# One input sum of a seven-product projection loaded after the last scores, and the second rope's scaling moved to ScalarE

## The chip, the cores and the metric

The kernel runs on one core of a Trainium2 chip. The metric is the time of one execution on the device in microseconds. Three runs of the kernel before gave 515.02, 515.41 and 516.37 us, so the median is 515.41 us. Engines are named as in the profile: PE is TensorE, PEld its weight loads, DVE VectorE, ACT ScalarE, POOL GpSimd and SP SyncE, from whose queue most transfers are issued.

## The reference

One decoder block over 512 tokens of 1024 channels, in float32. A projection of the normed input feeds two mixers: a sparse attention (compressed, selected and sliding branches) and a multi-scale retention of four heads, run in four chunks of 128 tokens. Their outputs are gated, merged, projected and added to the input. What matters here is the retention, and that attention's work precedes it:

```python
h = rms_norm(x, norm_pre)
proj = h @ w_in                              # 1024 -> 6936
(q_n, k_c, v_c, k_s, v_s, k_w, v_w, g_n, z_n,
 q_r, k_r, v_r, z_r, m_a, m_b) = jnp.split(proj, split_points(), axis=-1)
...
o_a = nsa_sequence(...)                      # attention, 8 heads of 64
y_a = (o_a * jax.nn.silu(z_n)) @ w_nsa_o
q_r = apply_rotary(q_r.reshape(B, S, 4, 128), ret_ang)
k_r = apply_rotary(k_r.reshape(B, S, 4, 128), ret_ang) * 128 ** -0.5
# retention, per chunk of 128 tokens and head:
att = jnp.einsum('nihd,njhd->nhij', qc, kc) * decay_mask
o = att @ v + (q * q_dec) @ state            # then state = decay * state + k^T v, o normalized
y_b = (o_b * jax.nn.silu(z_r)) @ w_ret_o
merged = jax.nn.sigmoid(m_a) * y_a + jax.nn.sigmoid(m_b) * y_b
return x + rms_norm(merged @ w_out, norm_post)
```

## The kernel before

A float32 product is made of three matmuls: each operand x is split into a high half `hi` in the matmul's reduced type (a copy, mostly on ACT, L200) and a low half `lo = x - hi` (a subtraction, mostly on DVE, L212), and PE adds hi·hi, hi·lo and lo·hi in one PSUM bank (`mm3`, whose matmuls are L233; transposes are L237). The normed and transposed input lies in `hTh` and `hTl`. Weights come from HBM through a ring of four `raw` tiles of 128 x 1024 (loads on SP, L373), and each half of a `raw` tile is split into `whi` and `wlo`, rings of nine. Working buffers are carved out of two large tiles: `arena_f` (float32) and `arena_r` (the matmul's type). `nat` is a ring of four tiles of 128 x 512 for intermediate results, `bank` a PSUM bank.

The program goes through a plan: after the first projections come the attention's blocks, then for the first pair of retention heads the rope (`QK`), values (`VR`) and gates, then `QZ2`: queries, keys and gates of the second pair of heads are computed in a Strassen-like way from seven products of half-size matrices instead of eight. Their names in the code are 11, s2 (with weight sum T2), s1 (T1), 22 (T4), 12, s4 and s3 (T3); those with an s need a sum of quarters of the input. The sums of the input (`hs` in DRAM) and of the weights (`wqT` and, for the later merge, `wmT`) are made by copies and accumulating transfers in DRAM on SP and POOL (L425, L434). `load_sum` brings an input sum into `arena_r`: one transfer from SP (L511), ACT makes the high half in place and the negated high half beside it (four steps of 128 x 512), and POOL issues a transfer that adds the source to the latter, which gives the low half. `free_at` says after which event the sum's buffer may be written. For the sum s2 (`qs2`) the buffer is the 8 KB of `arena_r` in which the low halves of the attention's keys, `kB`, lie; `att_head`, which issues the scores of one head and one block of 128 queries against `kA` and `kB`, is called 48 times.

`tail_qk` (L1134) is what follows the rope's products of one tile of 128 tokens. For the second pair of heads (`hp` = 1) it has a `base`: the tile's last product is added to an earlier partial sum (L212, `nat<-bank,arena_f`), and then four scaled products on half of the tile each (L225; a row's scale `rs` times the tile times the cosine or sine) and two combining steps (L212, `nat<-nat,nat`) give the roped queries and keys. PE transposes them (L237), ACT and DVE split them into halves, and `ret` computes the chunk's scores, masks them (ACT copies the scores' second half from the bank, DVE adds and masks, ACT makes the high half `ah`), multiplies them with the values and updates the state. `load_rtab` (L1132) loads the tables of cosine and sine, and the masks come at L1096 when the attention ends.

The order of all instructions on all queues is fixed when the program is built. A planner, `Order`, keeps a planned time for each engine and a list of generators, each of which says at what planned time and on which engine its next piece may go. The planner always records the piece that is first by those times. A piece which says that its data arrive later is therefore recorded later and placed further back on its engine's queue; what a piece is waiting for on the chip has no part in it. `e = od.dma(...)` is the planned landing of a transfer, and `yield e, "act"` hands the next piece to ACT's list with that time.

```python
    free_at = {"ms1": "ret13", "ms2": "MB0", "ms3": "P2", "ms4": "P1",
               "qs2": "att", "qs1": "vr01", "qs4": "qs2end", "qs3": "qs1end"}
```

Of the kernel before, what the change touches and what calls it, by code (L numbers as in the profile page):

```python
# [14 lines left out]
OP = mybir.AluOpType  # L15
# [3 lines left out]
P = 128  # L19
# [128 lines left out]
def block_kernel(ctx: ExitStack, tc, x, xT, g_pre, ws, small, w2s, norm_post, rope_r, dmask, out):  # L148
# [21 lines left out]
    def f(ap):  # L170
        return ap.bitcast(FT)
# [3 lines left out]
    od = Order()  # L175


    def size(a):
        n = 1
        for k in a.shape[1:]:  # L180
            n *= k
        return n
# [4 lines left out]
    def near(*aps):  # L187
        return not any(far(a) for a in aps)

    def act_ns(o, i, k=0):  # L190
        return 0.833 * size(o) + (51 if far(i) else 93) + 93 * k
# [4 lines left out]
    def lazy(*vals):  # L196
        return sum(v is not None and not isinstance(v, (int, float)) for v in vals)

    def act(o, i, func=AF.Copy, r=0.0, **kw):
        S.activation(o, i, func, **kw)  # L200
        return od.op("act", act_ns(o, i, lazy(kw.get("bias"), kw.get("scale"))) + (95 if "accum_out" in kw else 0), r)
# [9 lines left out]
    def tt(o, a, b, op, r=0.0, e="dve"):  # L211
        (V if e == "dve" else G).tensor_tensor(o, a, b, op=op)  # L212
        if op == OP.pow:
            return od.op(e, 300 + 164 * size(o), r, True)
        return od.op(e, (1.042 * size(o) + 69) if e == "dve" else (2.36 * size(o) + 77), r, e == "pool" or near(o, a, b))
# [8 lines left out]
    def stt(o, a, s, b, op0, op1, r=0.0):  # L224
        V.scalar_tensor_tensor(o, a, s, b, op0=op0, op1=op1)  # L225
        return od.op("dve", 1.042 * size(o) + 69 + 61 * lazy(s), r, near(o, a, b))
# [5 lines left out]
    def mm(ps, a, b, start, stop, r=0.0, cost=None):  # L232
        T.matmul(ps, a, b, start=start, stop=stop)  # L233
        return od.pe(cost or max(0.4418 * size(b) + 1, 107 if a.shape[-1] > 64 else 54), r, a.dtype == FT)

    def tr(ps, a, idn, r=0.0):
        T.transpose(ps, a, idn)  # L237
        return od.pe(58 if a.dtype == FR else 107, r, a.dtype == FT)
# [6 lines left out]
    def sub_split(lo, src, hi, r, e="dve"):  # L245
        return tt(lo, src, f(hi), OP.subtract, r, e)
# [98 lines left out]
    def h_quart(n):  # L345

        if n[0] == "q":
            return SQ[n in ("qs1", "qs3")]
        n = n.removeprefix("m")
        if n == "s1":  # L350
            return S1H, S1L
        k, c = hq[n]
        return hTh[:, k:k + 4, half[c]], hTl[:, k:k + 4, half[c]]

    free_at = {"ms1": "ret13", "ms2": "MB0", "ms3": "P2", "ms4": "P1",
               "qs2": "att", "qs1": "vr01", "qs4": "qs2end", "qs3": "qs1end"}

    def in_ring(p):

# [24 lines left out]
    nxt, freed = [0], {}  # L384
# [108 lines left out]
    def load_sum(key):  # L493

        yield od.need(free_at[key], "sum" + key[1:])
        r = max(freed[free_at[key]], sumr[id(hsum[key[1:]])])
        hi, lo = h_quart(key)
        src = hsum[key[1:]].rearrange("(p k c) -> p k c", p=P, k=4)
        yield r
        if key in ('qs3', 'qs4', 'ms2', 'ms3', 'ms4'):  # L500
            DMA.dma_start(f(lo), src)
            e = od.dma(P * 4096, r)
            for c in (slice(0, 2), slice(2, 4)):
                yield e, "act"
                act(hi[:, c], f(lo[:, c]), r=e)
            for c in (slice(0, 2), slice(2, 4)):
                yield od.eng["act"], "dve"
                sready[key] = sub_split(lo[:, c], f(lo[:, c]), hi[:, c], od.eng["act"])
            od.flags.add(key)
            return  # L510
        DMA.dma_start(f(hi), src)  # L511
        e = od.dma(P * 4096, r)
        for c in (slice(0, 2), slice(2, 4)):
            yield e, "act"
            act(hi[:, c], f(hi[:, c]), r=e)
            yield e, "act"
            ea = act(lo[:, c], f(hi[:, c]), r=e, scale=-1.0)
        ea = max(ea, adder[0])
        yield ea
        G.dma_start(lo.rearrange("p k c -> p (k c)"), src.rearrange("p k c -> p (k c)"), accum_op=OP.add)  # L520
        sready[key] = od.op("pool", 1000.0, ea) + 7000.0
        adder[0] = sready[key]
        od.flags.add(key)
# [124 lines left out]
    def rs(t, i=0):  # L648
        return rs3[:, i, t:t + 1]
# [310 lines left out]
    def att_head(t, g, brs, j, slot):  # L960

        L, nb, h, b0 = P * (t + 1), len(brs), g * 4 + j, brs[0]
        s = yield from PS.get()
        sv = s[:, 0:nb * L].rearrange("p (b c) -> p b c", b=nb)
        q = qT[t][:, h, :]
        mm(sv, q, kA[:, b0:b0 + nb, g, 0:L], True, False)
        e = mm(sv, q, kB[:, b0:b0 + nb, g, 0:L], False, True)
        yield e, "dve"

        Pj = slot["P"]  # L970
        pv = Pj[:, 0:nb * L].rearrange("p (b c) -> p b c", b=nb)
        nm, z = ((slot["stat"][:, i, j * nb:(j + 1) * nb]) for i in range(2))
        for b in range(nb):
            V.tensor_tensor_reduce(pv[:, b, :], sv[:, b, :], maskp[:, 512 - L:512], 1.0, -NEG, OP.add, OP.min,
                                   nm[:, b:b + 1])
            od.op("dve", 1.04 * L + 80, e)
        e = od.op("dve", 80)
        PS.put(s, e)
        yield e, "act"
        for b in range(nb):  # L980
            e = act(pv[:, b, :], pv[:, b, :], AF.Exp, r=e, bias=nm[:, b:b + 1], scale=-1.0, accum_out=z[:, b:b + 1])
        slot["pv"], slot["z"] = pv, e

    def att_norm(t, g, brs, slots):

# [137 lines left out]
    rtr = [0.0] * 8  # L1123

    def rtab_of(i):

        return rtab if i < 4 else zt[0][i - 4]

    def load_rtab(i, r):
        rtr[i] = od.dma(P * 2048, r)  # L1130
        od.flags.add(f"rt{i}")
        DMA.dma_start(rtab_of(i), rope_r[i // 4, i % 4 * P:(i % 4 + 1) * P, :])  # L1132

    def tail_qk(hp, t, ps, e, base=None):  # L1134
        yield od.need("q0", "q1", "q2", "q3", "cmp0", "cmp1", f"rt{4 * hp + t}")
        tv = rtab_of(4 * hp + t).rearrange("p (s a c) -> p s a c", s=2, a=4)
        t1 = yield from NAT.get()
        t2 = yield from NAT.get()
        v1 = t1.rearrange("p (a r c) -> p a r c", a=4, r=2)
        v2 = t2.rearrange("p (a r c) -> p a r c", a=4, r=2)  # L1140
        pv = v1 if base else ps.rearrange("p (a r c) -> p a r c", a=4, r=2)
        if base:
            u, given, then, *more = base
            yield od.need(given, *more)
            yield max(e, kept[given]), "dve"
            e = tt(t1, ps, u, OP.add, max(e, kept[given]))
            then(ps, e)
        yield max(e, rtr[4 * hp + t]), "dve"
        if not base:
            for i in range(2):  # L1150
                e = stt(v1[:, :, i, :], pv[:, :, i, :], rs(t), tv[:, 0], OP.mult, OP.mult, e)
            yield e, "dve"
        stt(v2[:, :, 0, :], pv[:, :, 1, :], rs(t), tv[:, 1], OP.mult, OP.mult, e)
        e = stt(v2[:, :, 1, :], pv[:, :, 0, :], rs(t), tv[:, 1], OP.mult, OP.mult, e)
        if base:
            yield e, "dve"
            for i in range(2):
                e = stt(v1[:, :, i, :], pv[:, :, i, :], rs(t), tv[:, 0], OP.mult, OP.mult, e)
        else:
            ACC.put(ps, e)  # L1160
        if hp == 0 and t < NT - 1:
            load_rtab(t + 1, e)
        yield e, "pool"
        tt(v1[:, :, 0, :], v1[:, :, 0, :], v2[:, :, 0, :], OP.subtract, e)
        e = tt(v1[:, :, 1, :], v1[:, :, 1, :], v2[:, :, 1, :], OP.add, e)
        NAT.put(t2, e)
        pt = yield from PT.get()
        yield e + PE_LAG
        act(kf[t], t1[:, 256:512], r=e)
        for a in range(4):  # L1170
            e = tr(pt[:, a * P:(a + 1) * P], t1[:, a * P:(a + 1) * P], ident)
        NAT.put(t1, e)
        yield e, "act"
        e = act(qk_h[t], pt, r=e)
        yield e, "dve"
        e = sub_split(qk_l[t], pt, qk_h[t], e)
        PT.put(pt, e)
        kr[t] = e
        od.flags.add(f"qk{hp}{t}")
# [60 lines left out]
    def pair_qz():  # L1240
# [18 lines left out]
        def keys(i, ps, e):  # L1259
            od.spawn(tail_qk(1, i, ps, e, (XA[i], f"qw{i}", free)), 1)  # L1260
# [589 lines left out]
    r = raws[0][1] - 600  # L1850
    for c in (slice(0, P), slice(P, SEQ)):
        e = act(hTh[:, 0, c], xTf[0][:, c], r=xTr[0], scale=gp[:, 0:1])
# [12 lines left out]
    for key in free_at:  # L1865
        od.spawn(load_sum(key), 1)
# [103 lines left out]
```

## Time and profile before

| What | Value |
|---|---|
| Median of three runs | 515.41 us (515.02 to 516.37) |
| Profiled execution | 515.82 us |
| Its span, first to last instruction | 513.9 us |
| Mean granted clock of PE | 0.996 |
| PE busy | 502.6 us (98%) |
| DVE busy | 424.2 us (83%) |
| ACT busy | 310.5 us (60%) |
| POOL busy | 49.7 us (10%) |

A line of the timeline gives the start and the length in microseconds, the engine, the line of the kernel, the operation, output and inputs, the shape and the number of instructions; a bracket at its end gives the engine's idle time just ahead and what ended it. A line of the grouped views has the count, then busy time in all and the mean in nanoseconds, then idle time ahead and its releasers. In the list of waits the numbers are total, times and longest. In the list of transfers the numbers are the size of one and the microseconds from its issue to its landing. Matmuls overlap, so that the start of the next one tells what one costs, not its length.

### The profile page before, as it was taken

To read this page: it belongs to the slowest core of one execution; us is meant where nothing else is said; L and a number is where in the kernel's file an instruction comes from. 1 tells how busy PE (TensorE), PEld (TensorE's weight loads), DVE (VectorE), ACT (ScalarE), POOL (GpSimd) and SP (SyncE) were. 2 spreads that over 40 slices of the span, in tenths; PEclk is the share of its full clock that TensorE was granted. 3 is DMA by queue.
4 is the path that set the end of the run, shared out by engine and by line. 5 is a ranking of instruction groups with operands and counts; after the bars stand their busy time and mean duration, and the time that the engine had idled before them with its cause. 6 is when DMAs were issued, how large, how long until landed. Compare 5 with 4: busy or idle time off the path is not lost.

```text
span 513.9 us, 7898 instructions
## 1 busy us (share of the span) xinstructions
PE 502.6 (98%) x2700; PEld 429.4 (84%) x2700; DVE 424.2 (83%) x987; ACT 310.5 (60%) x672; POOL 49.7 (10%) x82
## 2 busy tenths in 40 slices
PE   8999999999999999999999999999999999999994
PEld 7888789788888888888788887888888999888884
DVE  6699689979879789996689799786757789969887
ACT  5688579766568769575486575644614544427541
POOL 2000100000010000010131010113000000000011
PEclk9999999999999999999999999999999999999998
DMA  8997656702955732469669987185995997714825
GB/s 322 367 327 211 185 120 211 240 2 82 310 104 120 220 67 83 140 147 348 165 184 276 352 272 246 22 258 173 329 284 129 322 311 266 192 51 144 267 61 144
DMA packets 34248, 103.47 MB, mean 201 GB/s; under 512 B 3600, under 2 KB 8080, under 8 KB 34192
## 3 DMA queue, kind: packets, MB, share of 16 engines
q1 hardware_dynamic: 29312, 85.41, 46.3%
q0 software_dynamic: 4752, 17.30, 19.5%
q8 instruction: 21, 0.34, 0.3%
q10 hardware_dynamic: 144, 0.26, 0.1%
q14 instruction: 19, 0.16, 0.1%
HBM read 98.76 MB, written 34.08 MB: 259 GB/s over the span
## 4 chain that ended last, share of the span: by engine, by line
PE 80%; DVE 9%; DMA 5%; ACT 4%; issue 1%; SPq 0%; DVEq 0%; ACTq 0%
PE bank L233 75%; PE bank L237 5%; DMA arena_r<-hs 3%; DVE arena_f L212 2%; DVE wlo L212 2%; DVE arena_r L212 2%; ACT arena_r L200 2%; DMA raw<-in_stream_dram 1%; DVE nat L212 1%; ACT whi L200 1%; ACT nat L200 1%; DMA arena_f<-in_xT_dram 1%; DVE nat L225 1%; DVE arena_f L225 1%; ACT arena_f L200 0%
## 5 line engine op out<-in xcount | busy, mean ns | idle before, releaser
L200 ACT ACTIVATE whi<-raw 128x512 fp32r<-128x512 f32 x177 | 105.2, 627 | 53.7 <-PE bank L233 34.4
L212 DVE TENSOR_TENSOR wlo<-raw,whi 128x512 fp32r<-128x512 f32 x196 | 128.0, 686 | 9.2 <-ACT whi L200 6.5
L233 PE MATMUL bank<-whi,hTh 128*128 128x512 f32 x248 | 96.2, 403 | 0.3 <-ACT hTh L200 0.3
L233 PE MATMUL bank<-whi,hTl 128*128 128x512 f32 x248 | 93.3, 392 | 0.0
L233 PE MATMUL bank<-wlo,hTh 128*128 128x512 f32 x248 | 93.1, 391 | 0.0
L233 PE MATMUL bank<-arena_r 128*128 128x256 f32 (+2 forms) x328 | 69.5, 337 | 1.2 <-ACT arena_r L200 1.2
L233 PE MATMUL bank<-hTh,whi 128*128 128x512 f32 (+1 forms) x192 | 66.4, 346 | 0.0
L233 PE MATMUL bank<-arena_r,whi 128*128 128x512 f32 (+1 forms) x224 | 64.9, 374 | 0.0
L233 PE MATMUL bank<-hTh,wlo 128*128 128x512 f32 (+1 forms) x192 | 64.9, 338 | 0.0
L233 PE MATMUL bank<-hTl,whi 128*128 128x512 f32 (+1 forms) x192 | 64.9, 338 | 0.0
L233 PEld LDWEIGHTS bank<-arena_r 128*128 128x128 f32 x328 | 50.6, 189 | 7.7 <-ACT arena_r L200 1.6
L233 PEld LDWEIGHTS bank<-whi,hTl 128*128 128x128 f32 x248 | 46.5, 188 | 10.3 <-DVE hTl L225 0.3
L200 ACT ACTIVATE arena_r<-bank 128x512 fp32r<-128x512 f32 (+2 forms) x76 | 41.9, 569 | 21.6 <-PE bank L237 21.3
L233 PEld LDWEIGHTS bank<-whi,hTh 128*128 128x128 f32 x248 | 46.6, 188 | 9.1 <-ACT hTh L200 0.9
L233 PEld LDWEIGHTS bank<-wlo,hTh 128*128 128x128 f32 x248 | 46.7, 188 | 8.3
L200 ACT ACTIVATE arena_f<-arena_f,stat 128x384 f32<-128x384 f32 (+3 forms) x87 | 47.7, 560 | 8.2 <-DVE stat L212 4.6
L212 DVE TENSOR_TENSOR arena_r<-bank,arena_r 128x512 fp32r<-128x512 f32 (+2 forms) x68 | 43.7, 653 | 7.6 <-ACT arena_r L200 7.1
L233 PEld LDWEIGHTS bank<-arena_r,whi 128*128 128x128 f32 x224 | 41.0, 188 | 7.4
L233 PE MATMUL bank<-whi,arena_r 128*128 128x512 f32 (+1 forms) x152 | 44.7, 358 | 0.0
L233 PE MATMUL bank<-arena_r,wlo 128*128 128x512 f32 (+1 forms) x112 | 41.9, 374 | 0.0
L233 PEld LDWEIGHTS bank<-hTh,wlo 128*128 128x128 f32 x192 | 36.5, 190 | 4.0
L233 PEld LDWEIGHTS bank<-hTh,whi 128*128 128x128 f32 x192 | 36.5, 190 | 2.8
(160 smaller groups left out, 770.1 us busy)
## 6 DMA issues: line engine op xcount, KB each, us to landing
raw<-in_stream_dram SPq DMA_DIRECT2D x73, 512.0 KB, 4.8
arena_f<-in_xT_dram SPq DMA_DIRECT2D x16, 256.0 KB, 6.6
wqT<-in_stream_dram POOLq DMA_DIRECT2D x8, 512.0 KB, 5.4
raw<-wqT SPq DMA_DIRECT2D x8, 512.0 KB, 6.2
wmT<-in_stream_dram POOLq DMA_DIRECT2D x8, 512.0 KB, 7.4
woT<-in_stream_dram POOLq DMA_DIRECT2D x8, 512.0 KB, 7.6
raw<-wmT SPq DMA_DIRECT2D x8, 512.0 KB, 6.4
raw<-woT SPq DMA_DIRECT2D x8, 512.0 KB, 3.8
```

Source lines behind the costliest of these rows:

```text
L200: S.activation(o, i, func, **kw)
L212: (V if e == "dve" else G).tensor_tensor(o, a, b, op=op)
L225: V.scalar_tensor_tensor(o, a, s, b, op0=op0, op1=op1)
L233: T.matmul(ps, a, b, start=start, stop=stop)
L237: T.transpose(ps, a, idn)
```

## The change

Two edits. First, the flag on which the transfer of `qs2` waits is no longer the end of the attention but a new one, `scored`, which is set when the 48th `att_head` has recorded its score matmuls. The planned landing of that transfer gets 3000 ns more (the expression stands in both branches of `load_sum`, but `qs2` goes through the second alone). Second, `tail_qk` with a `base` no longer uses `rs` on DVE: ACT multiplies the sum by `rs` in place, DVE makes two plain products with the sine table (256 columns each) and one with the cosine table over all 512 columns, and the two combining steps stay. The tiles of the first pair are computed as before.

```diff
--- before.py
+++ after.py
@@ -353,7 +353,7 @@
         return hTh[:, k:k + 4, half[c]], hTl[:, k:k + 4, half[c]]
 
     free_at = {"ms1": "ret13", "ms2": "MB0", "ms3": "P2", "ms4": "P1",
-               "qs2": "att", "qs1": "vr01", "qs4": "qs2end", "qs3": "qs1end"}
+               "qs2": "scored", "qs1": "vr01", "qs4": "qs2end", "qs3": "qs1end"}
 
     def in_ring(p):
 
@@ -499,7 +499,7 @@
         yield r
         if key in ('qs3', 'qs4', 'ms2', 'ms3', 'ms4'):
             DMA.dma_start(f(lo), src)
-            e = od.dma(P * 4096, r)
+            e = od.dma(P * 4096, r) + (3000.0 if key == "qs2" else 0.0)
             for c in (slice(0, 2), slice(2, 4)):
                 yield e, "act"
                 act(hi[:, c], f(lo[:, c]), r=e)
@@ -509,7 +509,7 @@
             od.flags.add(key)
             return
         DMA.dma_start(f(hi), src)
-        e = od.dma(P * 4096, r)
+        e = od.dma(P * 4096, r) + (3000.0 if key == "qs2" else 0.0)
         for c in (slice(0, 2), slice(2, 4)):
             yield e, "act"
             act(hi[:, c], f(hi[:, c]), r=e)
@@ -965,6 +965,10 @@
         q = qT[t][:, h, :]
         mm(sv, q, kA[:, b0:b0 + nb, g, 0:L], True, False)
         e = mm(sv, q, kB[:, b0:b0 + nb, g, 0:L], False, True)
+        heads.append(e)
+        if len(heads) == 48:
+            freed["scored"] = e
+            od.flags.add("scored")
         yield e, "dve"
 
         Pj = slot["P"]
@@ -980,6 +984,8 @@
         for b in range(nb):
             e = act(pv[:, b, :], pv[:, b, :], AF.Exp, r=e, bias=nm[:, b:b + 1], scale=-1.0, accum_out=z[:, b:b + 1])
         slot["pv"], slot["z"] = pv, e
+
+    heads = []
 
     def att_norm(t, g, brs, slots):
 
@@ -1138,25 +1144,27 @@
         t2 = yield from NAT.get()
         v1 = t1.rearrange("p (a r c) -> p a r c", a=4, r=2)
         v2 = t2.rearrange("p (a r c) -> p a r c", a=4, r=2)
-        pv = v1 if base else ps.rearrange("p (a r c) -> p a r c", a=4, r=2)
+        pv = ps.rearrange("p (a r c) -> p a r c", a=4, r=2)
         if base:
             u, given, then, *more = base
             yield od.need(given, *more)
             yield max(e, kept[given]), "dve"
             e = tt(t1, ps, u, OP.add, max(e, kept[given]))
             then(ps, e)
-        yield max(e, rtr[4 * hp + t]), "dve"
-        if not base:
+            yield e, "act"
+            e = act(t1, t1, r=e, scale=rs(t))
+            r = max(e, rtr[4 * hp + t])
+            yield r, "dve"
+            for i in range(2):
+                tt(v2[:, :, i, :], v1[:, :, 1 - i, :], tv[:, 1], OP.mult, r)
+            e = tt(v1, v1, tv[:, 0].unsqueeze(2).broadcast_to([P, 4, 2, 64]), OP.mult, r)
+        else:
+            yield max(e, rtr[4 * hp + t]), "dve"
             for i in range(2):
                 e = stt(v1[:, :, i, :], pv[:, :, i, :], rs(t), tv[:, 0], OP.mult, OP.mult, e)
             yield e, "dve"
-        stt(v2[:, :, 0, :], pv[:, :, 1, :], rs(t), tv[:, 1], OP.mult, OP.mult, e)
-        e = stt(v2[:, :, 1, :], pv[:, :, 0, :], rs(t), tv[:, 1], OP.mult, OP.mult, e)
-        if base:
-            yield e, "dve"
-            for i in range(2):
-                e = stt(v1[:, :, i, :], pv[:, :, i, :], rs(t), tv[:, 0], OP.mult, OP.mult, e)
-        else:
+            stt(v2[:, :, 0, :], pv[:, :, 1, :], rs(t), tv[:, 1], OP.mult, OP.mult, e)
+            e = stt(v2[:, :, 1, :], pv[:, :, 0, :], rs(t), tv[:, 1], OP.mult, OP.mult, e)
             ACC.put(ps, e)
         if hp == 0 and t < NT - 1:
             load_rtab(t + 1, e)
```

ACT's queue, around the last scores and the attention's end. The four `arena_r<-arena_r` rows are the steps on the first input sum, `nat`, `arena_f` and `arena_r<-bank` are tails of the attention and the first rope.

```order
 L200 ACTIVATE arena_r<-bank_88 128x512
-L200 ACTIVATE whi<-raw 128x512 x3
+L200 ACTIVATE whi<-raw 128x512
+L200 ACTIVATE arena_r<-arena_r 128x512 x4
+L200 ACTIVATE whi<-raw 128x512
 L200 ACTIVATE nat_110<-bank_90 64x512
 L200 ACTIVATE arena_f<-nat_107 128x256
 L200 ACTIVATE whi<-raw 128x512 x2
 L200 ACTIVATE arena_r<-bank_87 128x512
-L200 ACTIVATE whi<-raw 128x512 x3
-L200 ACTIVATE arena_r<-arena_r 128x512 x4
+L200 ACTIVATE whi<-raw 128x512 x4
```

The four steps moved from behind the last of these splits to a place eight splits and tail rows earlier.

SP's queue over the same stretch (`wqT` copies are sums of weights, `hs_137` is the first input sum, `in_rope_r` the rope tables, `in_dmask` the retention masks).

```order
 L425 DMA wqT_134<-wqT_130 64x2x1024
 L425 DMA wqT_135<-wqT_131 64x2x1024
-L1132 DMA arena_f<-in_rope_r_dram 128x512 x2
-L373 DMA raw<-in_stream_dram 128x1024 x2
-L1096 DMA arena_f<-in_dmask_dram 128x4x128
 L511 DMA arena_r<-hs_137 128x1024
+L1138 DMA arena_f<-in_rope_r_dram 128x512 x2
+L373 DMA raw<-in_stream_dram 128x1024
+L1102 DMA arena_f<-in_dmask_dram 128x4x128
+L373 DMA raw<-in_stream_dram 128x1024
 L425 DMA wmT_120<-in_stream_dram 64x2x1024
```

The sum's load moved ahead of two rope tables, two weight loads and the masks. On POOL its accumulating transfer correspondingly stands one accumulation into `wqT_135` earlier.

DVE's queue at the first two key tiles of the second pair, in the kernel before (`nat_108` is the first tile's sum, `nat_107` the second's, `rs_146` the row scales; `arena_f<-nat_110,arena_f` is a gate).

```order
L212 TENSOR_TENSOR nat_108<-bank_84,arena_f 128x512
L212 TENSOR_TENSOR wlo<-raw,whi 128x512
L225 SCALAR_TENSOR_TENSOR arena_f<-nat_110,arena_f 128x512
L225 SCALAR_TENSOR_TENSOR nat_109<-nat_108,rs_146,arena_f 128x4x64 x2
L212 TENSOR_TENSOR wlo<-raw,whi 128x512
L212 TENSOR_TENSOR nat_107<-bank_85,arena_f 128x512
L225 SCALAR_TENSOR_TENSOR nat_108<-nat_108,rs_146,arena_f 128x4x64 x2
L225 SCALAR_TENSOR_TENSOR nat_110<-nat_107,rs_146,arena_f 128x4x64 x2
L212 TENSOR_TENSOR nat_108<-nat_108,nat_109 128x4x64 x2
```

And in the changed kernel, at the same place:

```order
L212 TENSOR_TENSOR nat_108<-bank_84,arena_f 128x512
L225 SCALAR_TENSOR_TENSOR arena_f<-nat_110,arena_f 128x512
L212 TENSOR_TENSOR wlo<-raw,whi 128x512
L212 TENSOR_TENSOR nat_109<-nat_108,arena_f 128x4x64 x2
L212 TENSOR_TENSOR nat_108<-nat_108,arena_f 128x512
L212 TENSOR_TENSOR nat_107<-bank_85,arena_f 128x512
L212 TENSOR_TENSOR wlo<-raw,whi 128x512
L212 TENSOR_TENSOR nat_108<-nat_108,nat_109 128x4x64 x2
```

The scaled products became plain ones, the cosine product became one row of 512 columns and stands directly behind the sine products, and the second tile's products moved behind the first tile's end. ACT's scaling of `nat_108` stands between the add and the first product, on another queue.

## The prediction

> **What bounds the kernel now.** I read the page first: its engine table, then its tenths.
>
> ```profile
> span 513.9 us, 7898 instructions
> ...
> PE 502.6 (98%) x2700; PEld 429.4 (84%) x2700; DVE 424.2 (83%) x987; ACT 310.5 (60%) x672; POOL 49.7 (10%) x82
> ```
>
> PE works 98% of the span, so only the moments in which PE stands still can be won. The change leaves the matmuls as they are; what it can be worth is therefore bounded by PE's waits in the stretch it touches. The list of PE's waits comes next.
>
> ```profile
> PE bank L233 <- ACT arena_r L200: 1.2, 1, 1.2
> ...
> PE bank L237 <- DVE arena_f L688: 0.9, 1, 0.9
> PE bank L237 <- DVE nat L212: 0.6, 1, 0.6
> ```
>
> The middle one lies at the start of the program (L688, the norm), which the change does not reach. The other two are at 245 us and 309 us; PE's timeline, with the rows just ahead of each, gives their size.
>
> ```profile
> 244.04 0.39 PE L233 MATMUL bank<-wlo,hTh 128*128 128x512 f32 x1
> 244.27 0.39 PE L233 MATMUL bank<-whi,hTl 128*128 128x512 f32 x1
> 245.83 1.91 PE L233 MATMUL bank<-arena_r 128*128 128x256 f32 x12 [1.17 <-ACT arena_r L200]
> ...
> 308.11 0.39 PE L233 MATMUL bank<-whi,hTl 128*128 128x512 f32 x1
> 309.06 0.66 PE L237 MATMUL bank<-ident,nat 128*128 128x128 f32 x4 [0.56 <-DVE nat L212]
> ```
>
> A matmul of 512 columns starts 0.23 us after the one ahead of it (244.04 to 244.27). Between 244.27 and 245.83 there are 1.56 us, so 1.33 are lost; between 308.11 and 309.06 there are 0.95, so 0.72 are lost. The two together, 2.05 us or 0.4%, are the most that the change can win directly. The chain of waits tells what is behind the first one.
>
> ```profile
> 232.79 0.63 SPq L1096
> ...
> 233.47 5.96 DMA arena_r<-hs
> ...
> 245.36 0.42 ACT arena_r L200
> ...
> 245.83 1.20 PE bank L233 x6
> ```
>
> The sum for the second Strassen product is issued at 233.47, takes 5.96 us, and ACT's work on it follows; after that come the retention tile's own (245.36 is its last, the high half of the masked scores), and PE gets it at 245.83.
>
> **The change, first part: the sum goes earlier.** The buffer's low halves of the keys are read last by the last scores, not by the end of the attention.
>
> ```profile
> 214.60 0.40 PE L233 MATMUL bank<-arena_r 128*128 128x256 f32 x2
> ...
> 214.93 1.19 SPq L425 DMA_DIRECT2D wqT<-wqT  x2
> 219.53 9.17 SPq L1132 DMA_DIRECT2D arena_f<-in_rope_r_dram  x2
> ```
>
> These are the last scores on PE and SP's rows behind them. The load now stands after the two copies of 214.93 and ahead of the rope loads, so it is issued at about 216.2. Its transfer shares the engines with the two copies; the groups of issues in that stretch price it:
>
> ```profile
> wqT<-wqT SPq DMA_DIRECT2D x2, 512.0 KB, 5.2
> arena_r<-hs SPq DMA_DIRECT2D x1, 512.0 KB, 6.0
> ...
> arena_r<-hs SPq DMA_DIRECT2D x2, 512.0 KB, 8.3
> ```
>
> The last row is of 274 to 286 us, where the same kind of load met four weight loads. 216.2 + 6.0 to 8.3 gives a landing at 222 to 225. ACT's four steps now stand behind a split of about 227:
>
> ```profile
> 227.80 1.31 ACT L200 ACTIVATE whi<-raw 128x512 fp32r<-128x512 f32 x2 [0.50 <-PE bank L233]
> ...
> 235.32 0.63 ACT L200 ACTIVATE whi<-raw 128x512 fp32r<-128x512 f32 x1 [2.56 <-DMA raw<-in_stream_dram]
> 239.45 2.48 ACT L200 ACTIVATE arena_r<-arena_r 128x512 fp32r<-128x512 f32 x4 [3.50 <-DMA arena_r<-hs]
> ```
>
> So they start 2 us or more after the landing and wait for nothing. They cost 2.48 us of ACT time there instead of here; behind them stand the splits of 227.80 and later, whose weights PE needs only some microseconds on, and ACT idles 2.56 us at 235.32, which takes up the push. I cost that at nothing; if this cover were gone, at most 2.48 us would fall on a split that PE waits for. The idle time of 3.50 us ahead of 239.45 goes with them.
>
> What is then last for the retention tile? Its scores on PE, and ACT's copy of them.
>
> ```profile
> 241.26 0.57 PE L233 MATMUL bank<-arena_r 128*128 128x256 f32 x4
> ...
> 243.50 0.38 ACT L200 ACTIVATE arena_f<-bank 128x256 f32<-128x256 f32 x1
> ```
>
> The order has the scores some five matmuls of 0.23 us nearer to the front, so at about 240.0 (239.8 to 240.2). They take 0.41 (241.26 to 241.67, the next start), and from ACT's copy to the end of the high half it is 245.36 + 0.42 − 243.50 = 2.28 us: 242.5 to 242.9. PE would ask at 244.27 + 0.23 = 244.50, or three matmuls sooner where the tile's products now stand, 243.8. That leaves about 1 us, and the first stall goes: −1.33 us.
>
> SP also moves two rope loads, raw loads and the mask load behind this one issue: 0.50 us of SP each time, no more; the rope loads, which stood at 219.53 waiting for their buffers for most of 9.17 us, lose nothing. POOL's accumulating load of the sum passes ahead of one accumulation into the weights' sums; those are read at 290 us or later. Both at nothing. The 3 us added to the planned landing costs nothing by itself: it only places ACT's steps.
>
> **Second part: ACT scales.** The rope of the second pair, four tiles, before and after on DVE (grouped by form, 280 to 320 us):
>
> ```profile
> L225 DVE SCALAR_TENSOR_TENSOR nat<-nat,rs,arena_f 128x256 f32<-128x256 f32 x16 | 6.8, 481 | 0.0
> ...
> L212 DVE TENSOR_TENSOR nat<-nat,nat 128x256 f32<-128x256 f32 x8 | 3.0, 420 | 0.0
> ...
> L200 ACT ACTIVATE arena_f<-arena_f,rs 128x512 f32<-128x512 f32 x4 | 2.9, 717 | 2.3 <-DVE arena_f L212 2.3
> ```
>
> Four scaled products of 256 columns go; in their place come two plain products of 256 and one of 512. On DVE's timeline the step from one start to the next tells what each costs:
>
> ```profile
> 298.88 0.69 DVE L212 TENSOR_TENSOR nat<-bank,arena_f 128x512 f32<-128x512 f32 x1
> 299.48 0.68 DVE L212 TENSOR_TENSOR wlo<-raw,whi 128x512 fp32r<-128x512 f32 x1
> ...
> 302.67 1.67 DVE L225 SCALAR_TENSOR_TENSOR nat<-nat,rs,arena_f 128x256 f32<-128x256 f32 x4
> 304.25 0.76 DVE L212 TENSOR_TENSOR nat<-nat,nat 128x256 f32<-128x256 f32 x2
> 304.92 1.29 DVE L212 TENSOR_TENSOR wlo<-raw,whi 128x512 fp32r<-128x512 f32 x2
> ...
> 308.25 0.75 DVE L212 TENSOR_TENSOR nat<-nat,nat 128x256 f32<-128x256 f32 x2
> ...
> 318.29 0.75 DVE L212 TENSOR_TENSOR nat<-nat,nat 128x256 f32<-128x256 f32 x2
> ```
>
> Four scaled products in a row cost 1.58 us (302.67 to 304.25), two plain ones of 256 columns 0.67 (304.25 to 304.92), one of 512 columns 0.60 (298.88 to 299.48). So 1.58 − 1.27 = 0.31 us less on DVE for each tile, 1.2 us in all, and 4 × 0.717 = 2.9 us more on ACT (the form's row with `rs`, the gates' scaling of the same size), off PE's path as long as DVE has other work between the add and the first product.
>
> DVE's rows carry no idle time from 298.88 to 319.04 (318.29 + 0.75): it, not the data, sets when the tiles are ready. I call the start of the first add X (298.88 before). The second tile is ready 10.1 us after X now. After, by the order, there stand eleven full-width instructions (0.60 each) and four pairs (0.67) between the first add and that tile's end: 9.3 us. PE asks for it at 308.34 − 1.33 = 307.0. With X one stall earlier (297.55) it is ready at 306.9 and the stall goes; with X unmoved it is ready at 308.2 and PE waits 1.2.
>
> The last tile: ready 20.2 us after X now, and PE takes it at 319.58 with 0.5 us to spare. After, four savings of 0.31 come off, but a gate's product and three more subtractions, 2.2 us together, are placed ahead of it: 21.1 to 21.2 us. PE's wish is 319.58 less 2.05, plus three matmuls (0.69) and a group of scores (0.41) that now stand ahead: 318.63. With X = 297.55 it is ready at 318.7, even.
>
> So all hangs on X, which DVE's and ACT's work of 280 to 298 us sets:
>
> ```profile
> 261.79 0.42 DVE L208 CAST whi<-raw 128x512 fp32r<-128x512 f32 x1
> 262.12 0.69 DVE L212 TENSOR_TENSOR wlo<-raw,whi 128x512 fp32r<-128x512 f32 x1
> ...
> 285.83 1.29 DVE L212 TENSOR_TENSOR arena_r<-arena_r 128x512 fp32r<-128x512 f32 x2 [1.86 <-ACT arena_r L200]
> ...
> 294.89 1.29 DVE L212 TENSOR_TENSOR arena_r<-arena_r 128x512 fp32r<-128x512 f32 x2 [1.15 <-ACT arena_r L200]
> ```
>
> In the order after, the high halves of three splits stand on DVE ahead of X, at 0.33 us for a cast (261.79 to 262.12): +1.0. Against it, the two idle times, 1.86 and 1.15 us, end with loads of other sums and may be filled by these same casts: −0.7 to −1.0. Lower bound of X 296.9 (idle gone, casts paid by it), upper 298.7 (casts in full, idle kept, shift of 1.33 by PE lost on the way). At the low end nothing is given back, at the high end 1.0 us or a little over. I take 297.6, nearest to the rows' balance, and 0.35 us given back between the two tiles.
>
> Sum: −1.33 − 0.72 + 0.35 = −1.70 us. The profiled execution took 515.82 us, its span being 513.9; so 514.1 for it. It stands 0.41 above the median of 515.41, and from that the forecast is 513.7, or −0.33%. About 0.3% (1.55 us) is what a measurement of this kernel can tell from no change, so the forecast lies just on the faster side of 513.86.
>
> One rule speaks against the second part. ACT needs 0.717 us where DVE saves 0.31; counted on the path, that is 4 × 0.41 = 1.6 us lost, and it is rival D below. I don't count it so, since ACT is busy 60% of the span and DVE 83%, and DVE has other rows to do in between. The Trainium skill, page "ScalarE: Activation LUTs", section "Rules for kernel authors", advises VectorE and not ScalarE for a plain add or multiply; by it the second part would be a loss. On the single instruction the trace agrees (0.717 us for 512 columns on ACT, 0.60 for a product of 512 on DVE).
>
> **The rivals.** A: the second part gives back what it was to win. X stays near 298.7, since the high halves on DVE and late landings hold it, and the stall at 309 stays or moves to a later tile: 515.41 − 1.33 + 0 to 0.5 = 514.1 to 514.6, within 0.3%. For it: DVE has no idle time in twenty microseconds, and X needs to follow a PE that is 1.33 us earlier. Against: 3.0 us of idle time just ahead.
>
> B: the change does not act at 245. Scores, not ACT, could set the tile's high half, or SP's issue stays behind the copies. Then 515.4. Against it: ACT's own 3.50 us wait and 214.60 for the scores.
>
> C, slower: the hop through ACT lengthens the key tiles, because a scale stands on ACT's queue behind a split whose load has not landed. A row of such a wait:
>
> ```profile
> 302.87 0.63 ACT L200 ACTIVATE whi<-raw 128x512 fp32r<-128x512 f32 x1 [1.43 <-DMA raw<-in_stream_dram]
> ```
>
> If that comes at a scale, DVE stands 1.43 + 0.72 us with the tile behind it, and each of the other three loses 0.72 − 0.31 = 0.41: 3.4 us in all on PE, with the stall of 309 kept. 515.41 − 1.33 + 3.4 = 517.5. It decides once the idle time of DVE ahead of its first product passes the 1 to 2 us that its other pieces fill.
>
> D: the hop alone is on the path, without a late landing: each of the four tiles loses 0.41 us, and nothing of the second stall is won. 515.41 − 1.33 + 1.6 = 515.7. It is what the rule of the Trainium skill named above would make of it. Against it: after the first add the order has two more full-width rows (1.2 us) ahead of the first product.
>
> **How the numbers follow.** The forecast 0.50, its own range 513.2 to 513.9 (between nothing and 0.5 given back of 2.05); A 0.28; B 0.07; C 0.09; D 0.06. Faster takes the forecast's share and the lower edge of A: 0.52. The rest of A, B, D and a weak form of C are within 0.3%: 0.40. C in full passes 516.96: 0.08. The range, 512.9 to 515.7, holds the forecast, A, B and D's centre, with 0.4 below for landing waits of the splits that also go.
>
> **What would show it.** In the profile after: no wait of PE on ACT at 245; SP's issue of the sum at about 216, its landing before 226, and ACT's four steps at 227 to 230 with no idle time ahead; then DVE's first add at about 297.6, PE's transposes of the second tile at about 307.0 without a wait, and of the last at 318.6 to 319.0. A wait of PE on DVE `nat` longer than 1 us there, or an idle DVE row released by ACT `nat`, means A or C. A landing of the sum later than 228, or a split after it that PE waits for, would make the first part wrong.

## The result and the profile after

The changed kernel takes 522.47 us, median of six runs (520.65 to 522.90), against 514.96 us of the kernel before in six runs (513.13 to 516.37). The ratio is 1.0139, with an interval from 1.0114 to 1.0165: slower by 1.4%, where 0.33% faster was forecast and 515.7 us was the end of the range. The profiled execution took 522.86 us, its span is 7.0 us longer than before.

The page's first lines and the list of PE's waits of the changed kernel:

```profile
span 520.9 us, 7897 instructions
...
PE 505.1 (97%) x2700; PEld 429.7 (83%) x2700; DVE 424.0 (81%) x984; ACT 311.5 (60%) x675; POOL 49.9 (10%) x82
```

```profile
PE bank L233 <- ACT whi L200: 3.0, 1, 3.0
PE bank L237 <- DVE nat L212: 1.7, 3, 0.7
...
PE bank L233 <- DVE wlo L212: 0.9, 2, 0.8
PE bank L237 <- DVE arena_f L212: 0.5, 1, 0.5
```

The wait of 1.2 us for ACT `arena_r`, which the first part was to remove, is gone from the list. A wait of 3.0 us for a split of weights (`whi`) is new, and it is not where the change is. Set side by side matmul by matmul (both profiles have 2700), the changed kernel is within 0.2 us until 230 us, 1.3 us behind at 353 us, still 1.3 us behind at 376 us, and 7.0 us behind from 394 us to the end. So 5.7 of the 7.0 us are lost between 378 and 387 us, early in the merge (the second Strassen-like computation). PE's timeline there:

```profile
378.41 0.39 PE L233 MATMUL bank<-arena_r,wlo 128*128 128x512 f32 x1
381.84 0.73 PE L233 MATMUL bank<-arena_r,whi 128*128 128x512 f32 x2 [3.04 <-ACT whi L200]
383.32 0.79 PE L233 MATMUL bank<-arena_r,wlo 128*128 128x512 f32 x1 [0.75 <-DVE wlo L212]
383.91 1.05 PE L233 MATMUL bank<-arena_r,whi 128*128 128x512 f32 x2
384.77 0.63 PE L233 MATMUL bank<-arena_r,wlo 128*128 128x512 f32 x1
```

PE waits 3.2 us for the first split and 0.9 for its low half, and then a matmul steps by 0.43 us (383.91 to 384.77 for two) where it takes 0.23. That is the lower level of the clock, as the windows of the same stretch show (the numbers are length, busy time of PE, PEld, DVE, ACT and POOL, then the granted clock, DMA share and GB/s):

```profile
360.00:380.00 20.00, 18.80 (x83) 15.21 (x81) 9.98 (x17) 8.62 (x16) 2.43 (x3) 1.00 0.99 306
380.00:390.00 10.00, 7.41 (x25) 5.71 (x26) 6.71 (x11) 3.65 (x7) 1.40 (x2) 0.83 0.92 236
```

The rest of the 5.7 us, some 1.6, is put down to the clock: 3.2 + 0.9 + 1.6 = 5.7. What ACT waited for stands on its timeline and on SP's:

```profile
366.83 2.47 ACT L200 ACTIVATE arena_r<-arena_r 128x512 fp32r<-128x512 f32 x4
380.12 1.15 ACT L200 ACTIVATE hTh<-hTl 128x512 fp32r<-128x512 f32 x2 [10.82 <-DMA hTl<-hs]
381.17 2.17 ACT L200 ACTIVATE whi<-raw 128x512 fp32r<-128x512 f32 x4
```

```profile
363.96 0.33 SPq L373 DMA_DIRECT2D raw<-in_stream_dram  x1
364.34 0.57 SPq L1471 DMA_DIRECT2D out_dram<-in_x_dram  x1
364.96 0.57 SPq L1472 DMA_DIRECT2D arena_f<-in_x_dram  x1
365.58 0.46 SPq L1473 DMA_DIRECT2D arena_f<-in_norm_post_dram  x1
366.14 0.60 SPq L501 DMA_DIRECT2D hTl<-hs  x1
```

ACT stood 10.82 us before its two steps on an input sum of the merge (`hTl<-hs`, called `ms2` in the code), and four splits stood behind them. On SP three loads for the end of the program (the copy of half the input to the output, the other input rows, the norm's weights) are issued ahead of that sum. In the kernel before they stand behind it:

```profile
362.34 0.61 SPq L501 DMA_DIRECT2D hTl<-hs  x1
363.00 0.68 SPq L1463 DMA_DIRECT2D out_dram<-in_x_dram  x1
...
369.78 1.13 ACT L200 ACTIVATE hTh<-hTl 128x512 fp32r<-128x512 f32 x2
```

Neither edit touches these rows. The planner records whatever is first by its planned times; part two alone makes the three loads' moment come first (e2 below), part one alone does not (e1). Which of its shifted times does it is not shown. From issue to landing the sum took 7.2 us before and 14.0 after.

### The profile page after: what moved, and what is told of

It is laid out like the page before. It is cut to its first block, busy times and chain, and to the rows that moved or that the text cites. A ratio compares the mean times of both kernels' runs of the same rounds, so it can differ in the third digit from the quotient of the medians.

```text
span 520.9 us, 7897 instructions
## 1 busy us (share of the span) xinstructions
PE 505.1 (97%) x2700; PEld 429.7 (83%) x2700; DVE 424.0 (81%) x984; ACT 311.5 (60%) x675; POOL 49.9 (10%) x82
## 4 chain that ended last, share of the span: by engine, by line
PE 69%; DVE 17%; DMA 9%; ACT 2%; issue 2%; SPq 0%; DVEq 0%; ACTq 0%
PE bank L233 64%; DVE wlo L212 4%; PE bank L237 4%; DVE arena_r L212 4%; DVE arena_f L212 3%; DMA hTl<-hs 3%; DVE nat L212 3%; DMA raw<-in_stream_dram 2%; DMA arena_f<-in_rope_r_dram 2%; DMA arena_r<-hs 1%; DVE nat L225 1%; ACT whi L200 1%; DVE arena_f L225 1%; ACT arena_r L200 1%; DMA arena_f<-in_xT_dram 1%
## 5 line engine op out<-in xcount | busy, mean ns | idle before, releaser
L233 PE MATMUL bank<-arena_r,whi 128*128 128x512 f32 (+1 forms) x224 | 66.0, 379 | 3.0 <-ACT whi L200 3.0
```

## The experiments

Theory T: the two edits themselves are about neutral, and the loss is the order of the queues at 360 to 380 us. Its rivals: the early transfer costs, the hop through ACT costs, and, within T, the loads' order alone or ACT's order alone is enough. Ratios are against the kernel before on the same chip.

| Run | Edit | Median us | Ratio | Interval |
|---|---|---|---|---|
| e1 | part one alone | 515.94 | 1.0011 | 0.9996 to 1.0025 |
| e2 | part two alone | 519.32 | 1.0081 | 1.0052 to 1.0110 |
| e3 | changed, final loads behind the sum | 516.15 | 1.0019 | 1.0006 to 1.0033 |
| e4 | before, final loads ahead of the sum | 515.07 | 1.0005 | 0.9986 to 1.0025 |
| e5 | part one, gate ahead of a split | 515.46 | 1.0018 | 1.0006 to 1.0030 |
| e6 | changed, sum's steps behind the splits | 515.87 | 1.0019 | 1.0006 to 1.0032 |
| e7 | changed, only the copy behind the sum | 515.92 | 1.0022 | 1.0009 to 1.0035 |
| e8 | part one without the 3000 ns | 518.40 | 1.0072 | 1.0051 to 1.0093 |
| e9 | part two, final loads behind the sum | 515.29 | 1.0003 | 0.9990 to 1.0015 |
| e10 | e3 and e5's exchange together | 516.15 | 1.0018 | 1.0006 to 1.0030 |
| e11 | e4, all four splits on ACT | 515.10 | 1.0001 | 0.9984 to 1.0018 |
| e12 | changed, POOL's accumulate later | 521.74 | 1.0141 | 1.0123 to 1.0159 |
| e13 | before against itself | 515.29 | 1.0019 | 1.0004 to 1.0034 |

The last row comes first in reading: the kernel before, compared with itself, shows 1.0019. So the 0.2% of e3, e5, e6, e7 and e10 are no difference that this comparison can tell, and the 0.3% of the prediction was near the least that could be seen.

**The parts apart.** e1 has the new flag, the counter and the 3000 ns; e2 has `tail_qk` as in the diff above and nothing else.

> Part one alone: the sum's load on the new flag, with the 3000 ns, DVE scaling as before. Theory (nearly all of the loss is the three loads of the final stage standing ahead of the merge's input sum on SP): this version has the sum ahead of them, as before, so no wait at 378 us; the stall at 245 goes (-1.33), a wait of the transposes at 240 comes (+0.83): 514.0 to 515.0, ratio 0.998 to 1.000. Rival (the earlier transfer itself costs, by contention or by ACT's steps in front of splits): 516.5 or more.

> Part two alone: ACT scales, the first sum loaded after the attention as before. Theory: this version has the three final loads ahead of the merge's sum, so it has the wait of 3 us or more at 378 with a lower granted clock behind it (+5.7), keeps the stall at 245, and its key tiles are no faster: 520 to 521.5, ratio 1.010 to 1.013. Rival (the early load is needed for the loss at 378): within 1 us of before.

e1 is the same as before within its interval, though a little above the range expected; the early transfer costs nothing that this comparison can tell. e2 loses 0.8%, and its profile has the same wait (PE on ACT `whi`, 2.3 us) with the sum landing after 13.0 us: part two alone turned the order round. It lost less than the 1.0% expected. Its profile is of the longest of the seven runs (523.82 us), so the sizes in it are not those of the median.

**The order of the loads.** In e3 the three loads wait, in the planner, for the sum's issue; in e4 it is the other way round in the kernel before.

```diff
 # e3, in ga_split and load_sum of the changed kernel
+        yield od.need("ms2sent")
         DMA.dma_start(out[0:2 * P, :], x[0:2 * P, :])
...
             DMA.dma_start(f(lo), src)
+            od.flags.add(key + "sent")
 # e4, in load_sum and ga_split of the kernel before
+            if key == "ms2":
+                yield od.need("fin")
...
+        od.flags.add("fin")
         DMA.dma_start(npost, ...)
```

> The changed kernel, with one edit: the three loads of the final stage are issued after the merge's input sum, as before. ACT's queue is that of the changed kernel, with the sum's steps ahead of four splits. Theory: 522.5 - 5.7 = 516.8, ratio 1.002 to 1.005, PE without a wait at 378, the sum landing in about 7 to 8 us. Rival (ACT's queue, with four splits behind the sum's steps where there were two, is the cause): 519 to 522.

> The kernel before, with one edit: the three loads of the final stage are issued ahead of the merge's input sum. Nothing else of the change. Theory: 515.0 + 5.7 = 520.7, ratio 1.009 to 1.012, with the wait at 378 and the clock at its lower level behind it. Rival (ACT's queue): two splits behind the sum's steps, so a smaller loss, 516 to 518.

e3 takes the whole loss away, with ACT's queue unchanged: the sum lands 7.0 us after its issue, and PE has no wait there. e4 does not bring it about: 1.0005 where 1.009 to 1.012 was expected. In its profile (516.33 us, 1.3 above its median) the sum landed late (12.7 us), but PE waited only 1.4 us, lost 1.7 in all, and kept its clock:

```profile
375.57 1.15 ACT L200 ACTIVATE hTh<-hTl 128x512 fp32r<-128x512 f32 x2 [8.38 <-DMA hTl<-hs]
376.63 1.14 ACT L200 ACTIVATE whi<-raw 128x512 fp32r<-128x512 f32 x2
...
378.79 0.50 PE L233 MATMUL bank<-arena_r,wlo 128*128 128x512 f32 x1 [1.36 <-DVE wlo L212]
```

So the loads ahead are needed for the loss in the changed kernel and, in the order of the kernel before, not enough. In e4 two splits stand behind ACT's steps, in the changed kernel four; the other two are casts on DVE in the kernel before, at 372.02, free of ACT's wait. The planner decides that split by split, by which engine would be done with it first in planned time.

**The other conditions.** e6 leaves SP's queue as changed and moves only ACT's two steps behind the four splits, by 6000 ns on that one sum's planned landing; e7 moves only the 1 MB copy behind the sum.

```diff
 # e6, in the first branch of load_sum
-            e = od.dma(P * 4096, r) + (3000.0 if key == "qs2" else 0.0)
+            e = od.dma(P * 4096, r) + (6000.0 if key == "ms2" else 0.0)
 # e7, in ga_split
-        DMA.dma_start(out[0:2 * P, :], x[0:2 * P, :])
+        od.spawn(copy_x(), 1)       # waits for "ms2sent", then issues the same copy
```

> The changed kernel with ACT's two steps on the merge's input sum placed behind the four splits that followed them (6000 ns on the planned landing of that one sum). SP's queue is unchanged: the three final loads stay ahead. Theory (two conditions together: the sum lands late, and four splits stand behind its ACT steps): PE has its weights, no wait at 378, 516 to 517.5, ratio 1.001 to 1.004. Rival (the bytes on the DMA engines make the weights themselves late): 520 or more.

> The changed kernel with only the copy of the first half of the input into the output (DRAM to DRAM, 1 MB) behind the merge's sum on SP; the two other final loads of 512 KB each stay ahead. Theory (the landing is late by the bytes that stand ahead): the sum lands in 9 to 11 us where it took 13.95, so the wait shrinks to nothing or 1.5 us: 516.5 to 518.5. Rival (the copy runs beside and the loads into the same engines' memory count): landing as late as now, 520 or more.

Both cure it whole. The landings, from the lists of issues of e6 and of e7 (KB, median us to landing):

```profile
hTl<-hs SPq DMA_DIRECT2D x1, 512.0 KB, 13.7
...
out_dram<-in_x_dram SPq DMA_DIRECT2D x1, 8.3
```

```profile
hTl<-hs SPq DMA_DIRECT2D x1, 512.0 KB, 8.4
out_dram<-in_x_dram SPq DMA_DIRECT2D x1, 10.7
```

In e6 the sum is as late as in the changed kernel, and nobody minds: the splits stand ahead of its steps on ACT, and PE keeps the upper clock (1.00 from 360 to 390 us). ACT's timeline of e6:

```profile
372.23 1.99 ACT L200 ACTIVATE whi<-raw 128x512 fp32r<-128x512 f32 x3 [3.87 <-PE bank L233]
380.27 0.63 ACT L200 ACTIVATE whi<-raw 128x512 fp32r<-128x512 f32 x1 [6.05 <-DMA raw<-in_stream_dram]
380.81 1.14 ACT L200 ACTIVATE hTh<-hTl 128x512 fp32r<-128x512 f32 x2
```

So PE was never short of weights in `raw`; it was short of an engine to split them. Between these two profiles the copy's place alone makes 5.3 us of the landing, which came sooner in e7 than the 9 to 11 us expected.

> The kernel before with both conditions made by hand: the three final loads ahead of the merge's sum (as in the earlier run that lost 1.7 us at 378 by its profile), and the two splits that DVE makes there given to ACT, so that four stand behind ACT's steps on the sum. Theory (both together starve PE): a wait of 1.2 us for ACT's split and 0.9 for DVE's low half at 376 to 379, 2.1 us without the lower clock, 3.5 to 4 with it: 516.5 to 518.8, ratio 1.003 to 1.008. Rival (the place of the splits does not matter once the sum is late): as the earlier run, ratio 1.000 to 1.002.

e11 is e4 with the casts of splits 133 and 134 given to ACT (`act` in place of `cp_any`), to make both conditions by hand. It loses nothing. In its profiled execution the same six issues on SP as in e4 gave a landing after 9.3 us and not 12.7:

```profile
hTl<-hs SPq DMA_DIRECT2D x1, 512.0 KB, 9.3
out_dram<-in_x_dram SPq DMA_DIRECT2D x1, 6.6
```

How late is too late follows from the timelines. In the changed kernel PE could have taken the split at 378.6 (378.41 and a step of 0.23), 12.5 us after the sum's issue; ACT needs 1.7 us from the landing to the end of the first split behind it (380.12 to 381.80), so a landing within 10.8 us would have cost nothing at that split. Its low half, which PE took 3.2 us after the landing (383.32) and would have taken at 379.1, asks for about 1 us less. Both are estimates from this one profile. In e11 PE took that matmul at 376.3, 13.3 us after the issue, so by the same 1.7 us it had 11.6. The flights were 14.0 in the changed kernel, 13.0 in e2, 13.4 in e12 (below), and 9.3 in e11: the first three pass the limit, the last doesn't. The single run of 518.52 us among e11's ten (the others end at 516.57) may be an execution in which the flight passed it; no profile shows it. So e11's profile has only one of the two conditions, and that both together bring the loss into the kernel before is not shown.

> The changed kernel with one accumulating transfer into the output projection's weight sum (woT<-in_stream on POOL, issued at 362.74 and landed at 369.12, beside the six loads of SP) put behind the merge's own accumulate on POOL. SP's and ACT's queues up to 385 us are those of the changed kernel. Theory (three things together make the sum late: the final loads ahead, this accumulate beside them, and the splits behind ACT's steps): the sum lands 9.3 to 12.7 us after its issue, as in the two runs of the kernel before with the loads ahead, and not after 14; the wait at 378 shrinks to 0 to 2 us and the clock keeps its upper level: 516 to 519, ratio 1.002 to 1.007. Rival (the loads ahead alone make 14 us): 520.5 or more.

e12 put an accumulating transfer of POOL (`woT`) behind the merge's own, since it ran beside the six loads in the changed kernel alone. The rival won: 1.0141, a flight of 13.4 us, the same wait (2.4 us). Why the flight is 13 to 14 us in the changed schedule and 9.3 to 12.7 in the old one, with the same six issues in the same order, stays open.

**Where the first part's gain went.** e1's profile has no wait at 245, and a new one at 283. On ACT the normalized output of the last retention tile (two rows, `arena_f<-bank,nm,rv`) stands behind a split whose load is late, and its transposes wait:

```profile
280.77 0.63 ACT L200 ACTIVATE whi<-raw 128x512 fp32r<-128x512 f32 x1 [3.91 <-DMA raw<-in_stream_dram]
281.31 1.00 ACT L200 ACTIVATE arena_f<-bank,nm,rv 128x256 f32<-128x256 f32 x2
...
283.09 0.66 PE L237 MATMUL bank<-ident,arena_f 128*128 128x128 f32 x4 [1.45 <-DVE arena_f L212]
```

e5 exchanges just these two pieces on ACT (split 96 waits, in the planner, for the gate's flag). e10 does the same to e3.

> Part one alone with one pair of ACT rows exchanged: the normalized output of the last retention tile of the first pair (arena_f<-bank,nm,rv) stands ahead of the split that waited 3.91 us for its weights at 276 to 280 us, and not behind it. Theory (part one wins its 1.3 to 1.6 us at 245 and loses it again at 281, where the tile's transposes wait for that row): no wait of PE at 281, 514.2 to 514.8, ratio 0.997 to 0.999. Rival (PE is ahead of its weights in this stretch anyway, and another wait takes the place): 515.5 to 516, ratio 1.000 to 1.001.

> The changed kernel with both repairs: the final loads behind the merge's sum, and the last retention tile's normalized output ahead of the late split on ACT. Theory (DVE sets the pace of 280 to 320 us, so a wait of PE that is removed ahead of it comes back at the key tiles' transposes, as in the run with part one): no wait at 281, longer ones at 303 to 322, 515 to 516, ratio 1.000 to 1.002. Rival (DVE is 1.2 us lighter here, so the gain stays): 513.8 to 514.5, ratio 0.997 to 0.999.

The wait at 283 is gone in both, and both are no faster: it stands one consumer on, at the key tiles' transposes. So e5's theory (0.997 to 0.999) failed, and e10's held. PE's timeline of e5 and of e10:

```profile
304.17 0.66 PE L237 MATMUL bank<-ident,nat 128*128 128x128 f32 x4 [0.95 <-DVE nat L212]
```

```profile
304.32 0.63 PE L237 MATMUL bank<-ident,nat 128*128 128x128 f32 x4 [0.83 <-DVE nat L212]
320.77 0.63 PE L237 MATMUL bank<-ident,nat 128*128 128x128 f32 x4 [0.47 <-DVE nat L212]
```

DVE sets the pace up to 320 us: its rows carry no idle time from 286 to 320 us in either profile. An earlier PE only arrives earlier at DVE's results, and ACT's scaling does not change that by what could be measured.

> Part two alone, with the three final loads kept behind the merge's sum as in the kernel before: what the scaling on ACT costs by itself. Theory (it takes as much from PE's waits as it gives; the loss of part two was all in the loads' order): the stalls at 245 and at the second tile stay, no wait at 378, 514.5 to 515.8, ratio 0.999 to 1.002. Rival (the hop through ACT costs on each of four tiles): 516.5 to 517, ratio 1.003 or more.

e9 is part two with e3's edit: 1.0003. The hop through ACT is neutral within its interval.

> Part one alone without the 3000 ns on the planned landing. ACT's four steps on the first sum stand some five rows earlier, ahead of tails of the attention. The transfer landed at 222.43 in the changed kernel, so these rows wait on ACT's queue until then. Theory (the 3000 ns matter only for ACT's wait there): a wait of ACT of 1 to 3 us at 219 to 222, of which PE sees 0 to 1: 515.5 to 517, ratio 1.000 to 1.003. Rival (the later rows' order, which differs from then on, decides): outside of that.

e8 has no wait of ACT where it was expected: the four steps stand at 224.07 and the data are there. It loses 0.7% all the same, with PE waiting 1.9 us for DVE `arena_r` near 365 us, at the merge's start, and a mean granted clock of 0.72 from 364 to 370 us. The rival was right: the 3000 ns act through the later order, not through ACT's wait.

## Why the prediction was wrong

**The step that failed** is the sum's end. It closed with the key tiles at 320 us and put everything behind at nothing, without a sentence on it. On SP it followed the moved transfer past the rope tables, the weight loads and the masks, and stopped. The order of the changed kernel had the three final loads ahead of the merge's sum, and ACT's steps on that sum ahead of four splits where there had been two. Both were fixed when the program was built, and no rival named them. That is 5.7 of 7.0 us in the profiled execution, and the whole difference by e3, e6 and e7. What the runs showed in its place is a sum that lands 14.0 us after its issue, ACT idle for 10.82 us ahead of its steps, and PE without the split behind them for 3.2 us.

**The first stall**: the mechanism was right, the size was of one execution. The transfer was issued at 216.10, ACT's four steps stood at 227.10 without idle time, and no wait of PE on ACT `arena_r` is left. But the 1.33 us were taken from one profile. The same rows of the unchanged schedule at 245 us, in a second profile of the kernel before (e13) and in e4:

```profile
245.16 1.92 PE L233 MATMUL bank<-arena_r 128*128 128x256 f32 x12 [0.35 <-ACT arena_r L200]
...
308.10 0.66 PE L237 MATMUL bank<-ident,nat 128*128 128x128 f32 x4 [0.28 <-DVE nat L212]
```

```profile
244.57 1.92 PE L233 MATMUL bank<-arena_r 128*128 128x256 f32 x12 [0.58 <-ACT arena_r L200]
```

Against 1.17 and 0.56 us of idle time in the profile that the prediction used, e13 has 0.35 and 0.28. In e2 the first was 1.76. The 2.05 us, the most that could be won, was thus the size of one execution; e13's profile would have made it about 1.

**What is late next** at 245 was answered with "about 1 us" of slack, and the tile behind the next late load was not looked for. ACT's gate at 281 (1.45 us in e1) is that.

**X**, the first add of the key tiles, was put at 297.6 with bounds of 296.9 and 298.7. In the changed kernel's profile:

```profile
240.40 0.66 PE L237 MATMUL bank<-ident,nat 128*128 128x128 f32 x4 [0.68 <-DVE nat L212]
...
299.92 0.67 DVE L212 TENSOR_TENSOR nat<-bank,arena_f 128x512 f32<-128x512 f32 x1
...
305.21 0.63 PE L237 MATMUL bank<-ident,nat 128*128 128x128 f32 x4 [0.60 <-DVE nat L212]
...
321.65 0.63 PE L237 MATMUL bank<-ident,nat 128*128 128x128 f32 x4 [0.47 <-DVE nat L212]
```

X is later than the upper bound. As the bound is worded (casts in full, idle time kept, PE's shift lost) it comes to 298.88 + 1.0 = 299.9 and not to 298.7, and there X stands. The late gate at 281 holds DVE up for 1.19 us in this profile, but it isn't what sets X: in e10 that wait is gone, and X is still at 299.00. From 280 to 300 us DVE has 32 instructions and 17.9 us of work in both, against 28 and 16.7 in the kernel before. From X to the last tile's transposes it is 21.7 us, against the 21.1 to 21.2 worked out plus a hop: the chain's length was about right, its start was not.

So the term of 0.35 us given back was too small. The stall at 309 is gone, but the first key tile now waits 0.60 us and the last 0.47. With 0.53 us at the gate (282.83) and the 0.68 at 240.40, which no other profile with the early sum has, these waits (2.28 us) are more than the 1.17 and 0.56 us that went; this profile is 1.3 us behind before the merge begins. In e5 and e10 the gain is given back at the key tiles, as rival A has it (it was given 0.28); in e1 and e3 most of it is lost ahead of them, at the gate.

**Rival D and the rule.** By it each key tile would lose 0.41 us. e9 shows 1.0003, from 0.9990 to 1.0015, so the 1.6 us (0.3%) it gives is outside the interval, if not by much beside the 0.2% of the null comparison. The prediction's 0.717 us against 0.60 for the single instruction compares a length with a step, and the 0.60 is an add's. Length against length it is 0.725 us for ACT's scaling and 0.692 for DVE's product of 512 columns in the changed kernel, hardly a difference. The Trainium skill, page "ScalarE: Activation LUTs", section "Rules for kernel authors", prefers VectorE for a plain multiply; the runs here show no loss from ACT, in a stretch where DVE is the busier engine.

## What to carry to other kernels

Where a planner orders the queues, a change has two effects, what it does in its place and what the new order does everywhere behind it, and the second was the larger here (5.7 us in the profile, against a difference too small to tell in e3, e6 and e7). Read the whole difference of order to the program's end, queue by queue, and ask of each in-order engine what stands behind an instruction whose data come later now; a wait that no one needed becomes one for everything queued behind it. Before a wait is priced as a gain, take its size from two or three executions, and ask which engine paces the stretch behind it.

## What the runs showed of the hardware

The flight of a 512 KB load, issued behind the same loads on the same queue, was 12.7 us in one execution (e4) and 9.3 in another (e11); in two executions of the kernel before, whose sum is issued ahead of them, it was 7.2 and 5.7 (e13). With a copy of 1 MB from DRAM to DRAM ahead of it on the queue it was 13.7 us (e6), with the copy behind it 8.4 (e7), one profile each. With an accumulating transfer of another queue out of its way it was 13.4 and not 14.0 (e12), a difference smaller than that between two executions. After 3 us without matmuls and a second pause of 0.75, PE's steps went from 0.23 to 0.43 us for some 2 us; after e4's single pause of 1.36 us they did not, and in e2's profile, after a single pause of 1.76 us that ended at 247 us, they did (the granted clock of 249 to 251 us was 0.50). The kernel before against itself gave 1.0019, with an interval that leaves out 1, so a ratio of 1.002 here is nothing.
